# The beginning of a layer rebuilt: the first norm's scale spread by TensorE, the rotary tables computed on GpSimd, half of the key-value product between the indexer's blocks

## The chip, the cores and the metric

The kernel runs on one core of a Trainium2 chip. A core has five engines, each with an instruction stream of its own that runs in order: TensorE (PE, matmuls and transposes), VectorE (DVE), ScalarE (ACT), GpSimd (POOL) and SyncE (SP, which here issues the DMAs). They wait for each other through semaphores. The metric is the time of one execution on the device in microseconds (us); the median of several runs is given.

## The reference

The input (512 tokens of width 1024, float32) goes through a first layer norm and then through two hybrid decoder layers, each of which is, cut to what matters:

```python
x = layer_norm(x, ln_in_g, ln_in_b)            # once, ahead of both layers
h = x @ w_in                                   # 1704 columns: qa ka va qb kb vb qi ki wi
qa, ka, qb, kb, qi = (rope(...) for each)      # rotary by cos/sin of position * frequency
ki = rope(layer_norm(ki, idx_k_g, idx_k_b))
oa = swa_sink_attention(qa, ka, va, sinks)     # window of 128, 8 heads, 2 key heads
score = sum_h relu(qi_h . ki) * wi_h           # the indexer: 8 heads of width 32
sel = top_k(causal score, 128)
ob = attention of qb over the selected kb, vb  # 8 heads, 1 key head
x = layer_norm(ALPHA * x + concat(oa, ob) @ w_o, ln1_g, ln1_b)
ffn = (silu(x @ w_g) * (x @ w_u)) @ w_down     # 2816 wide
ple = (p @ w_pp) * sigmoid(x @ w_pg)
x = layer_norm(ALPHA * x + ffn + ple, ln2_g, ln2_b)
```

## The kernel before

**Tiles.** The 512 tokens are four tiles of 128 (x0 to x3, on partitions). `to_features(t)` turns a tile by eight PE transposes (L340), and ACT and DVE write it as a high half `fh` (L342) and a low half `fl` (L343). Every product is done in float32 as three matmuls of halves (`mm3`: L252 high by high, L253 high by low, L254 low by high).

**Weights.** SP loads a piece of weights into one of three `wst` buffers; ACT casts its high half (L228) and POOL subtracts for the low half (L229) into one of five `wsp` buffers. `w_pump` does this ahead of use, and `w_rel` gives a buffer back once the last product that uses it has been written.

**The beginning of a layer.** In layer 0, `ln_in(t)` norms a tile: statistics (L301, L306), the inverse root by a few operations on one column (L283 to L293), and two passes of multiply and add with scale and shift (`lng`, `lnb`), which are loaded as rows spread over 128 partitions. Tile 0 does this in two DVE operations of 1024 columns (L309, L316); tiles 1 to 3 do the first pass's upper half on POOL (L311, L312) and the rest on DVE (L313, L319). `rotary()` computes the angles of all positions, takes them down to one period by fourteen DVE operations (L370, L371, L376), and fills the tables `tab64` and `tab32` after ACT's sines (L379, L380). `start()` then does, for each tile, the 296 columns of the indexer ("the group": 24 matmuls a tile), then the 384 columns of keys and values ("key-value", tiles 0 and 1 first, then 2 and 3: 48 matmuls each), and two blocks of queries. In layer 1 the tiles 0 to 2 are turned at the end of layer 0 and only tile 3 is turned in `start()`.

**What follows.** Each product is rotated: `rope` multiplies by the table on DVE (L402), adds the halves (L404), then ACT makes the high half (L407) and POOL the low one (L408). `turn` transposes the result on PE (L414), and ACT copies it out (L415). `index()` multiplies index queries and keys for tiles 1, 2 and 3 (eight matmuls each of 256, 384 and 512 columns, L547), ACT takes the relu, and DVE accumulates in `work` (L550). `topk()` then finds the 128 largest of every row in sixteen rounds of eight (L561, L562) and makes the mask (L564), on DVE; the sparse attention of a tile waits for it. The attention runs after, and `w_o` closes the stretch.

**What sets the order.** `Order.run` interleaves streams that yield their PE cost; `later` puts a turn off by some microseconds of it. The code order that this gives is then rearranged by the framework's scheduler, engine by engine, so the final order of an engine isn't the order of the code. All PSUM tiles share eight banks.

## Time and profile before

| | |
|---|---|
| median of 3 runs | 1331.31 us (1329.1 to 1331.56) |
| the profiled execution | 1331.07 us |
| its span | 1329.2 us |
| PE busy | 1269.0 us (95%) |
| DVE busy | 620.0 us (47%) |
| POOL busy | 563.5 us (42%) |
| ACT busy | 510.6 us (38%) |

The span is what the profiler recorded of that execution, from the first to the last instruction; the execution's own time is 1.87 us longer. The busy shares are means over stages of very different kind: in the feed-forward part PE alone is full, while in the stretch from the start to `w_o` several engines are. The rows further down are of that stretch. [...]

### The profile page before, as it was taken

The numbers are of one execution on the slowest core, as the hardware profiler recorded it, in microseconds if no ns is written. First come the engines' busy times: TensorE is split into PE (matmuls) and PEld (weight loads), VectorE is DVE, ScalarE is ACT, GpSimd is POOL, SyncE is SP. The second block draws the span as 40 slices with busy tenths as digits, with TensorE's granted clock in tenths as the row PEclk, the third lists the DMA queues.
The fourth block names the chain that finished last, engine by engine and source line by source line (L and its number), as shares of the span: only waits on it lengthen the run. The fifth ranks groups of instructions, "written<-read, shape, count | busy, mean of one in ns | idle before, by whom it ended". The sixth has DMA issues, their size and how long they took to land.

```text
span 1329.2 us, 17760 instructions
## 1 busy us (share of the span) xinstructions
PE 1269.0 (95%) x6744; PEld 1098.4 (83%) x6744; DVE 620.0 (47%) x1532; ACT 510.6 (38%) x1052; POOL 563.5 (42%) x366
## 2 busy tenths in 40 slices
PE   2899999999999999999998999999999999999996
PEld 2899889788888888888897998989888888888885
DVE  7899956812120012122688998674121102121166
ACT  1566766333221132223246576743232212222220
POOL 5565332344444444443055534324444444444422
PEclk9899999999999999999998999998999999999999
DMA  5322110233332332234032210204333333232221
GB/s 183 95 80 70 44 33 32 84 100 102 96 111 95 95 95 96 95 96 136 19 105 84 91 33 33 64 13 130 96 98 100 117 97 95 96 95 95 95 79 48
DMA packets 88645, 113.77 MB, mean 86 GB/s; under 512 B 4848, under 2 KB 65264, under 8 KB 88560
## 3 DMA queue, kind: packets, MB, share of 16 engines
q1 hardware_dynamic: 88560, 112.64, 26.6%
q8 instruction: 53, 0.87, 0.3%
q14 instruction: 32, 0.26, 0.1%
HBM read 110.53 MB, written 2.10 MB: 85 GB/s over the span
## 4 chain that ended last, share of the span: by engine, by line
PE 85%; DVE 12%; ACT 1%; issue 1%; DMA 1%; SPq 0%; DVEq 0%; ACTq 0%
PE bank L252 26%; PE bank L253 26%; PE bank L254 26%; PE bank L586 2%; PE bank L630 2%; DVE t2k L404 2%; DVE work L562 1%; DVE m L561 1%; DVE t2k L402 1%; PE bank L624 1%; DVE t2k L589 1%; PE bank L547 1%; PE bank L414 1%; DVE fl L343 1%; DVE x L332 1%
## 5 line engine op out<-in xcount | busy, mean ns | idle before, releaser
L229 POOL TENSOR_TENSOR wsp<-wst,wsp 128x1024 fp32r<-128x1024 f32 (+2 forms) x190 | 450.7, 2377 | 535.7 <-ACT wsp L228 535.4
L228 ACT CAST wsp<-wst 128x1024 fp32r<-128x1024 f32 (+2 forms) x190 | 194.6, 1027 | 459.9 <-PE bank L254 288.8
L253 PE MATMUL bank<-fl,wsp 128*128 128x512 f32 (+1 forms) x768 | 286.9, 374 | 1.7 <-DVE fl L343 1.7
L254 PE MATMUL bank<-fh,wsp 128*128 128x512 f32 (+1 forms) x768 | 286.6, 374 | 0.0
L252 PE MATMUL bank<-fh,wsp 128*128 128x512 f32 (+1 forms) x768 | 285.4, 375 | 1.0 <-ACT fh L342 1.0
L786 DVE TENSOR_TENSOR t2k<-bank,t2k 128x512 f32<-128x512 f32 x44 | 30.0, 691 | 356.5 <-PE bank L254 356.5
L252 PE MATMUL bank<-wsp,slot 128*128 128x512 f32 x432 | 169.2, 392 | 0.0
L253 PEld LDWEIGHTS bank<-fl,wsp 128*128 128x128 f32 x768 | 146.7, 191 | 27.2 <-DVE fl L343 2.2
L254 PE MATMUL bank<-wsp,fl 128*128 128x256 f32 (+3 forms) x512 | 165.6, 325 | 3.5 <-DVE fl L343 3.5
L253 PE MATMUL bank<-wsp,slot 128*128 128x512 f32 x432 | 168.2, 389 | 0.0
L254 PE MATMUL bank<-wsp,slot 128*128 128x512 f32 x432 | 168.1, 389 | 0.0
L252 PE MATMUL bank<-wsp,fh 128*128 128x256 f32 (+3 forms) x512 | 166.8, 329 | 0.9 <-ACT fh L342 0.5
L252 PEld LDWEIGHTS bank<-fh,wsp 128*128 128x128 f32 x768 | 145.4, 191 | 26.5 <-ACT fh L342 1.9
L254 PEld LDWEIGHTS bank<-fh,wsp 128*128 128x128 f32 x768 | 146.6, 191 | 25.0
L253 PE MATMUL bank<-wsp,fh 128*128 128x256 f32 (+3 forms) x512 | 165.8, 324 | 0.1
L254 PEld LDWEIGHTS bank<-wsp,fl 128*128 128x128 f32 x512 | 99.2, 194 | 9.2 <-DVE fl L343 4.2
L252 PEld LDWEIGHTS bank<-wsp,fh 128*128 128x128 f32 x512 | 98.8, 194 | 7.9 <-ACT fh L342 1.4
L253 PEld LDWEIGHTS bank<-wsp,fh 128*128 128x128 f32 x512 | 99.5, 194 | 5.8 <-POOL wsp L229 0.4
L254 PEld LDWEIGHTS bank<-wsp,slot 128*128 128x128 f32 x432 | 81.1, 188 | 16.9
L253 PEld LDWEIGHTS bank<-wsp,slot 128*128 128x128 f32 x432 | 81.1, 188 | 16.2
L252 PEld LDWEIGHTS bank<-wsp,slot 128*128 128x128 f32 x432 | 81.1, 188 | 16.1
L707 DVE SCALAR_TENSOR_TENSOR x<-x,bank 128x512 f32<-128x512 f32 x32 | 21.8, 684 | 117.5 <-PE bank L254 117.5
(150 smaller groups left out, 1737.4 us busy)
## 6 DMA issues: line engine op xcount, KB each, us to landing
wst<-in_w_gu_dram SPq DMA_DIRECT2D x88, 512.0 KB, 3.4
wst<-in_w_down_dram SPq DMA_DIRECT2D x44, 512.0 KB, 3.6
wst<-in_w_in_dram SPq DMA_DIRECT2D x16, 512.0 KB, 3.5
wst<-in_w_o_dram SPq DMA_DIRECT2D x16, 512.0 KB, 3.6
wst<-in_w_pg_dram SPq DMA_DIRECT2D x16, 512.0 KB, 3.7
wst<-in_w_in_dram SPq DMA_DIRECT2D x8, 296.0 KB, 4.0
x<-in_x_dram SPq DMA_DIRECT2D x4, 512.0 KB, 8.7
wst<-in_w_in_dram SPq DMA_DIRECT2D x8, 256.0 KB, 2.8
```

The lines of the kernel that those rows point to most:

```text
L228: A.copy(w[:, 0, :a * n], st[:, :a * n])
L229: G.tensor_tensor(w[:, 1, :a * n], st[:, :a * n], w[:, 0, :a * n], OP.subtract)
L252: PE.matmul(o, sh, mh, start=start, stop=False)
L253: PE.matmul(o, sh, ml, start=False, stop=False)
L254: PE.matmul(o, sl, mh, start=False, stop=stop)
L332: V.scalar_tensor_tensor(xt[t], xt[t], rs, b_t, op0=OP.mult, op1=OP.add)
L343: V.tensor_tensor(fl[:, 4 * j:4 * j + 4, ts], pv, fh[:, 4 * j:4 * j + 4, ts], OP.subtract)
L404: V.tensor_tensor(t1.rearrange("p n (u i) -> p n u i", u=2), t1.rearrange("p n (u i) -> p n u i", u=2), t2.rearrange("p n (u i) -> p n u i ...
L586: PE.matmul(ps[:, o:o + nn], qT[kind, t, g][:, j * 128:(j + 1) * 128], kT[c, s][:, k0:k0 + nn], start=(s == 0), stop=(s == 1))
L630: PE.transpose(ps[:, j * 128:(j + 1) * 128], es[j][:, b * 128:(b + 1) * 128], idf)
L707: V.scalar_tensor_tensor(xt[t][:, c], xt[t][:, c], scale, ps, op0=OP.mult, op1=OP.add)
L786: V.tensor_tensor(b, ps[1, f], a, OP.mult)
```

## The change

- **Loads.** The positions and frequencies go first, x0 comes in two halves, and the first norm's scale and shift come as two tiles of 8 by 128 (`gb8`), in place of two rows spread over 128 partitions. x1 to x3 are issued inside `w_pump`, behind weight pieces 1, 3 and 4 (`X_AT`). The group's weights come in three pieces (3, 3 and 2 blocks of 128 rows) instead of four. The small rows of the indexer's norm and the sinks are issued after the rotary.
- **First norm.** Sixteen matmuls of a column of the identity, broadcast, by `gb8` put scale and shift on all partitions in four PSUM banks. `ln_in` does every tile in four DVE operations of 512 columns that read those banks; POOL has no part in it any more. `ln_apply` stays for the last norm only.
- **Rotary.** All its reduction runs on POOL, each multiply-add as two operations (24 in place of DVE's 14), and the table copies go from POOL to ACT.
- **Order of a layer's beginning.** The key-value product of tiles 0 and 1 runs after the group of tile 1 (layer 0) or of tile 2 (layer 1), ahead of the remaining groups. The key-value weights of the upper four row blocks go into `slot` tiles, their low halves still by POOL. `ln_in(t + 1)` is issued after tile t has been turned. `project` now takes weight pieces of unequal length and is told how many of them to give back.
- **ln1's scale** (`load_gb(("1", l))`) is loaded ahead of the attention rather than after it, held in the order of the program.

```diff
@@ -139,22 +139,26 @@
     def load_x(t):
-        SP.dma_start(xt[t], x[0, t * 128:(t + 1) * 128, :])
-    load_x(0)
+        for c in (slice(0, 512), slice(512, D)) if t == 0 else (slice(0, D),):
+            SP.dma_start(xt[t][:, c], x[0, t * 128:(t + 1) * 128, c])
     SP.dma_start(posi, bass.AP(tensor=positions.tensor, offset=positions.offset, ap=[[1, 128], [128, NT]]))
     bcast_row(invf, inv_freq, 0, 48)
+    load_x(0)
+    gb8 = t2k()
+    for i, row in enumerate((ln_in_g, ln_in_b)):
+        SP.dma_start(gb8[:KT, i * 128:(i + 1) * 128],
+                     bass.AP(tensor=row.tensor, offset=row.offset, ap=[[128, KT], [1, 128]]))
     gb = {}
     def load_gb(key, g_ap, b_ap, off):
...
         b_t = const.tile([128, D], F32, name="lnb", tag="lnb")
-        bcast_row(g_t, g_ap, off, D)
-        bcast_row(b_t, b_ap, off, D)
+        for dst, src in ((g_t, g_ap), (b_t, b_ap)):
+            tc.keep_in_program_order(bcast_row(dst, src, off, D))
         gb[key] = (g_t, b_t)
-    load_gb("in", ln_in_g, ln_in_b, 0)
-    load_x(1)
     wq = []
@@ -168,10 +172,10 @@
     for l in range(L):
+        for k, a in ((0, 3), (3, 3), (6, 2)):
+            plan(a, rows(w_in[l], k, a, QI, NIN))
         for k in range(0, KT, 2):
-            plan(2, rows(w_in[l], k, 2, QI, NIN))
-        for k in range(0, KT, 2):
-            plan(2, rows(w_in[l], k, 2, KA, KA + 256), rows(w_in[l], k, 2, KB, KB + 128))
+            plan(2, rows(w_in[l], k, 2, KA, KA + 256), rows(w_in[l], k, 2, KB, KB + 128), extra=k >= 4 and G)
         for c in (QA, QA + 256, QB, QB + 256):
@@ -209,6 +214,8 @@
                 wst_live[wpos["dma"]] = st
+                if wpos["dma"] in X_AT:
+                    load_x(X_AT[wpos["dma"]])
                 wpos["dma"] += 1
@@ -217,10 +224,10 @@
                 if extra:
-                    w = [[slot() for _ in range(a)] for _ in range(2)]
+                    w = [[slot()[:, :n] for _ in range(a)] for _ in range(2)]
                     for k in range(a):
                         A.copy(w[0][k], st[:, k * n:(k + 1) * n])
-                        V.tensor_tensor(w[1][k], st[:, k * n:(k + 1) * n], w[0][k], OP.subtract)
+                        extra.tensor_tensor(w[1][k], st[:, k * n:(k + 1) * n], w[0][k], OP.subtract)
                     w_live[i] = w
@@ -264,10 +267,16 @@
     V.tensor_copy(win[:, 128:], causal[:, S - 128:])
...
+    gb_in = []
+    for i in range(2):
+        for j in range(2):
+            ps = bank("gb", 4)
+            for k in range(KT // 2):
+                PE.matmul(ps[:, k * 128:(k + 1) * 128], idf[:KT, 4 * j + k, None].to_broadcast([KT, 128]),
+                          gb8[:KT, i * 128:(i + 1) * 128], start=True, stop=True)
+            gb_in.append(ps)
     def tok(t):
@@ -300,25 +309,30 @@
         V.bn_stats(stats[t][:, h, :], xt[t][:, h * 512:(h + 1) * 512])
...
+    def ln_in(t):
+        mv = sm(2, "bmv")
+        for h in range(2):
+            ln_stats(t, h)
+        V.bn_aggr(mv, stats.pop(t))
+        halves = [xt[t][:, h * 512:(h + 1) * 512] for h in range(2)]
+        for h, c in enumerate(halves):
+            V.scalar_tensor_tensor(c, c, mv[:, 0:1], gb_in[h], op0=OP.subtract, op1=OP.mult)
+        rs = rstd_of(mv[:, 1:2])
+        for h, c in enumerate(halves):
+            V.scalar_tensor_tensor(c, c, rs, gb_in[2 + h], op0=OP.mult, op1=OP.add)
@@ -342,15 +356,8 @@
             V.tensor_tensor(fl[:, 4 * j:4 * j + 4, ts], pv, fh[:, 4 * j:4 * j + 4, ts], OP.subtract)
-    def ln_in(t):
-        for h in range(2):
-            ln_stats(t, h)
-        ln_apply(t, "in")
-    ln_in(0)
-    V.tensor_copy(posf, posi)
+    G.tensor_copy(posf, posi)
...
     def rotary():
         n = NT * 48
...
+        ang, kk, aa, pr = t2k(), t2k(), t2k(), t2k()
         a3 = ang[:, :n].rearrange("p (t f) -> p t f", t=NT)
...
         for period, bits, terms in ((2 * math.pi * 4096, 7, 6), (2 * math.pi, 11, 4)):
-            V.tensor_scalar(kk[:, :n], ang[:, :n], 1.0 / period, magic, op0=OP.mult, op1=OP.add)
-            V.tensor_scalar(kk[:, :n], kk[:, :n], magic, None, op0=OP.subtract)
+            G.tensor_scalar(kk[:, :n], ang[:, :n], 1.0 / period, magic, op0=OP.mult, op1=OP.add)
+            G.tensor_scalar(kk[:, :n], kk[:, :n], magic, None, op0=OP.subtract)
             rest = period
...
                 rest -= c
-                V.scalar_tensor_tensor(ang[:, :n], kk[:, :n], -c, ang[:, :n], op0=OP.mult, op1=OP.add)
+                G.tensor_scalar(pr[:, :n], kk[:, :n], -c, None, op0=OP.mult)
+                G.tensor_tensor(ang[:, :n], pr[:, :n], ang[:, :n], OP.add)
         lim = 3.1415925
@@ -383,12 +391,18 @@
         for tab, f0, h in ((tab64, 0, 32), (tab32, 32, 16)):
-            G.tensor_copy(tab[:, :, 0, :h], c3[:, :, f0:f0 + h])
-            G.tensor_copy(tab[:, :, 0, h:], c3[:, :, f0:f0 + h])
-            G.tensor_copy(tab[:, :, 1, :h], s3[:, :, f0:f0 + h])
+            A.copy(tab[:, :, 0, :h], c3[:, :, f0:f0 + h])
+            A.copy(tab[:, :, 0, h:], c3[:, :, f0:f0 + h])
+            A.copy(tab[:, :, 1, :h], s3[:, :, f0:f0 + h])
             G.tensor_scalar(tab[:, :, 1, h:], s3[:, :, f0:f0 + h], -1.0, None, op0=OP.mult)
+    w_pump()
+    ln_in(0)
     rotary()
@@ -716,20 +728,21 @@
...
         def start():
-            ws = take(4)
+            gi, kv = take(3), []
             for t in range(NT):
-                if l == 0 and t > 0:
-                    ln_in(t)
                 if l == 0 or t == 3:
...
                     yield 0.9
-                yield from project(ws, 296, (t,), from_f, gi_out, t == 3)
-            ws = take(4)
-            for b in ALL:
-                yield from project(ws, 384, b, from_f, kv_out, b is ALL[-1])
+                if l == 0 and t + 1 < NT:
+                    ln_in(t + 1)
+                yield from project(gi, 296, (t,), from_f, gi_out, 3 * (t == 3))
+                if t == (1 if l == 0 else 2):
+                    kv = take(4)
+                    yield from project(kv, 384, ALL[0], from_f, kv_out)
+            yield from project(kv, 384, ALL[1], from_f, kv_out, 2)
             for q in QS[:NSTART]:
@@ -741,19 +754,19 @@
...
         order.run((start(), 1.0), (index(), 1.0))
+        load_gb(("1", l), ln1_g, ln1_b, l * D)
         order.run((rest(), R_MAIN), (attention(), 1.0), (topk(), R_TOP))
         order.flush()
-        load_gb(("1", l), ln1_g, ln1_b, l * D)
         wo = [take(2), take(2)]
```

How the order moves is seen at three places. In the rows, `x_85` to `x_88` are tiles 0 to 3, and lines of the new kernel are L354 (turn a tile to features), L255 to L257 (the three matmuls of `mm3`), L428 (turns of index queries), L525 (turns of keys), L559 (index product), L310 (statistics), L316 (their mean), L319 and L322 (the two passes of the norm).

PE of layer 0 around the first index product, before: key-value matmuls, turns, index product of tile 1, turns, index product of tile 2.

```order
L252 MATMUL bank<-wsp,fh 128x384
L253 MATMUL bank<-wsp,fh 128x384
L254 MATMUL bank<-wsp,fl 128x384
L414 MATMUL bank<-idr,slot 128x128 x10
L547 MATMUL bank<-slot 128x256 x8
L414 MATMUL bank<-idr,slot 128x128 x18
L547 MATMUL bank<-slot 128x384 x8
L252 MATMUL bank<-wsp,fh 128x384
```

The same place after the change:

```order
L255 MATMUL bank<-slot,fh 128x384
L256 MATMUL bank<-slot,fh 128x384
L257 MATMUL bank<-slot,fl 128x384
L354 MATMUL bank<-idf,x_87 128x128 x8
L428 MATMUL bank<-idr,slot 128x128 x10
L559 MATMUL bank<-slot 128x256 x8
L255 MATMUL bank<-wsp,fh 128x296
L256 MATMUL bank<-wsp,fh 128x296
L257 MATMUL bank<-wsp,fl 128x296
```

The first index product now stands right behind tile 2's transposes and half of the key-value product, and ahead of the groups of tiles 2 and 3 (the 296-column matmuls).

PE of layer 0 at the index products of tile 3, before: they stand one by one among the key-value matmuls.

```order
L253 MATMUL bank<-wsp,fh 128x384
L547 MATMUL bank<-slot 128x512
L254 MATMUL bank<-wsp,fl 128x384
L252 MATMUL bank<-wsp,fh 128x384
L253 MATMUL bank<-wsp,fh 128x384
L254 MATMUL bank<-wsp,fl 128x384
L252 MATMUL bank<-wsp,fh 128x384
L253 MATMUL bank<-wsp,fh 128x384
L547 MATMUL bank<-slot 128x512
```

After:

```order
L255 MATMUL bank<-wsp,fh 128x256
L256 MATMUL bank<-wsp,fh 128x256
L257 MATMUL bank<-wsp,fl 128x256
L428 MATMUL bank<-idr,slot 128x128 x10
L559 MATMUL bank<-slot 128x384 x8
L559 MATMUL bank<-slot 128x512 x8
L525 MATMUL bank<-idr,slot 128x128 x12
L255 MATMUL bank<-wsp,fh 128x256
L256 MATMUL bank<-wsp,fh 128x256
L257 MATMUL bank<-wsp,fl 128x256
```

The eight products of tile 2 and the eight of tile 3 now form one row, behind a block of query matmuls and ten turns.

DVE at the first norm of layer 0, before (`lng`, `lnb` are the spread rows):

```order
L306 BN_AGGR bmv<-bst 128x2
L292 TENSOR_SCALAR lnt_158<-lns_157,lnv_156 128x1
L376 SCALAR_TENSOR_TENSOR t2k<-t2k 128x192
L313 SCALAR_TENSOR_TENSOR x_86<-x_86,bmv,lng 128x512
L283 TENSOR_SCALAR lnv_263<-bmv 128x1
L293 TENSOR_SCALAR lns_157<-lnt_158,lns_157 128x1
L376 SCALAR_TENSOR_TENSOR t2k<-t2k 128x192
L286 TENSOR_SCALAR lns_264<-lnv_263 128x1
L316 SCALAR_TENSOR_TENSOR x_85<-x_85,lns_157,lnb 128x1024
L370 TENSOR_SCALAR t2k<-t2k 128x192
```

After (`bank` are the PSUM banks with scale and shift):

```order
L319 SCALAR_TENSOR_TENSOR x_85<-x_85,bmv,bank 128x512
L302 TENSOR_SCALAR lns_197<-lnt_198,lns_197 128x1
L310 BN_STATS bst<-x_86 128x6 x2
L322 SCALAR_TENSOR_TENSOR x_85<-x_85,lns_197,bank 128x512
L316 BN_AGGR bmv<-bst 128x2
L319 SCALAR_TENSOR_TENSOR x_86<-x_86,bmv,bank 128x512 x2
L292 TENSOR_SCALAR lnv_284<-bmv 128x1
L310 BN_STATS bst<-x_87 128x6 x2
L322 SCALAR_TENSOR_TENSOR x_85<-x_85,lns_197,bank 128x512
L310 BN_STATS bst<-x_88 128x6 x2
```

The statistics of tile 1 (and of tiles 2 and 3) now stand among tile 0's passes, and the rotary steps (L376, L370) are gone from between them.

## Rows read from the trace of the kernel before

**Rows 1.** The page, parts 1 and 4: busy time, share of the span and instructions of each engine; shares of the chain of work that ended last, by engine.

```profile
PE 1269.0 (95%) x6744; PEld 1098.4 (83%) x6744; DVE 620.0 (47%) x1532; ACT 510.6 (38%) x1052; POOL 563.5 (42%) x366
...
PE 85%; DVE 12%; ACT 1%; issue 1%; DMA 1%; SPq 0%; DVEq 0%; ACTq 0%
```

**Rows 2.** Windows of layer 0's first stretch: the window, its length, then busy us (instructions) of PE, PEld, DVE, ACT and POOL, PE's granted clock, the DMA share and GB/s.

```profile
20.00:40.00 20.00, 13.78 (x65) 12.08 (x64) 19.16 (x53) 5.60 (x11) 15.09 (x15) 0.91 0.38 107
40.00:60.00 20.00, 16.85 (x114) 16.68 (x114) 19.64 (x65) 8.07 (x18) 13.66 (x16) 1.00 0.35 104
60.00:80.00 20.00, 17.00 (x75) 15.09 (x76) 15.50 (x46) 13.79 (x39) 4.84 (x10) 0.74 0.10 28
160.00:180.00 20.00, 16.60 (x92) 13.48 (x93) 14.12 (x53) 14.11 (x51) 5.12 (x9) 1.00 0.08 27
```

**Rows 3.** Timeline of PE in layer 0: start, duration, engine, line, operation, operands, count, and in brackets the idle time before and what ended it.

```profile
18.08 1.97 PE L340 MATMUL bank<-idf,x 128*128 128x128 f32 x8 [18.08 <-DVE x L316]
...
24.26 0.62 PE L254 MATMUL bank<-wsp,fl 128*128 128x296 f32 x1 [3.53 <-DVE fl L343]
...
32.70 1.55 PE L340 MATMUL bank<-idf,x 128*128 128x128 f32 x8 [2.65 <-DVE x L319]
...
38.93 1.04 PE L340 MATMUL bank<-idf,x 128*128 128x128 f32 x8
...
48.26 0.34 PE L252 MATMUL bank<-wsp,fh 128*128 128x384 f32 x1
...
56.09 0.96 PE L414 MATMUL bank<-idr,slot 128*128 128x128 f32 x10
60.91 1.42 PE L547 MATMUL bank<-slot 128*128 128x256 f32 x5 [3.86 <-ACT slot L415]
```

**Rows 4.** Timeline of DVE in layer 0, same columns: x0's statistics, its first multiply, an early rotary step, its last multiply, three additions of the ropes, the first operation of topk(1) and the last one of topk(3).

```profile
4.52 1.29 DVE L301 BATCH_NORM_STATS2 bst<-x 128x6 f32<-128x512 f32 x2 [2.56 <-DMA x<-in_x_dram]
...
9.22 1.28 DVE L309 SCALAR_TENSOR_TENSOR x<-x,bmv,lng 128x1024 f32<-128x1024 f32 x1 [2.97 <-DMA lng<-in_ln_in_g_dram]
...
11.13 0.35 DVE L376 SCALAR_TENSOR_TENSOR t2k<-t2k 128x192 f32<-128x192 f32 x1
...
16.75 1.27 DVE L316 SCALAR_TENSOR_TENSOR x<-x,lns,lnb 128x1024 f32<-128x1024 f32 x1
...
47.83 3.83 DVE L404 TENSOR_TENSOR t2k<-t2k 128x64 f32<-128x64 f32 x3
...
66.55 0.43 DVE L561 MAX8 m<-work 128x8 f32<-128x256 f32 x1
...
170.41 0.43 DVE L564 TENSOR_SCALAR work<-work 128x512 f32<-128x512 f32 x1
```

**Rows 5.** Waits of PE in 690:830 (layer 1): engine, line, what it waited for, us in total, times, longest.

```profile
PE bank L547 <- ACT slot L415: 5.0, 1, 5.0
```

**Rows 6.** Windows of layer 1's first stretch, columns as in rows 2.

```profile
700.00:720.00 20.00, 14.69 (x75) 13.09 (x74) 16.60 (x57) 12.55 (x36) 7.69 (x13) 0.74 0.16 50
708.00:712.00 4.00, 3.71 (x20) 2.77 (x19) 3.27 (x8) 3.30 (x10) 0.00 (x0) 0.50 0.00 0
712.00:716.00 4.00, 4.00 (x16) 3.52 (x15) 3.40 (x11) 3.94 (x12) 1.33 (x3) 0.50 0.00 0
800.00:820.00 20.00, 17.99 (x113) 15.22 (x111) 19.74 (x69) 15.43 (x54) 9.85 (x14) 1.00 0.16 54
```

**Rows 7.** The page, part 6: DMA issues of the x tiles, count, KB each, median us from issue to landing.

```profile
x<-in_x_dram SPq DMA_DIRECT2D x4, 512.0 KB, 8.7
```

**Rows 8.** Timeline of ACT in layer 0, columns as in rows 3: the two fh casts of x2.

```profile
39.57 1.07 ACT L342 CAST fh<-bank 128x512 fp32r<-128x512 f32 x2 [0.25 <-PE bank L340]
```

**Rows 9.** Groups of DVE's instructions in 0:66, by line and shape: busy us, mean ns of one, idle time before them.

```profile
L376 DVE SCALAR_TENSOR_TENSOR t2k<-t2k 128x192 f32<-128x192 f32 x10 | 7.8, 776 | 0.0
...
L343 DVE TENSOR_TENSOR fl<-bank,fh 128x512 fp32r<-128x512 f32 x8 | 5.4, 678 | 0.6 <-ACT fh L342 0.6
...
L319 DVE SCALAR_TENSOR_TENSOR x<-x,lns,lnb 128x512 f32<-128x512 f32 x6 | 4.9, 869 | 0.0
```

**Rows 10.** Groups of POOL's instructions in 0:56, same columns.

```profile
L311 POOL TENSOR_SCALAR x<-x,bmv 128x512 f32<-128x512 f32 x3 | 5.6, 1882 | 0.4 <-DVE bmv L306 0.4
...
L312 POOL TENSOR_TENSOR x<-x,lng 128x512 f32<-128x512 f32 x3 | 3.8, 1272 | 0.0
...
L381 POOL TENSOR_TENSOR t2k<-t2k 128x192 f32<-128x192 f32 x1 | 0.5, 501 | 0.0
...
L382 POOL TENSOR_SCALAR t2k<-t2k 128x192 f32<-128x192 f32 x1 | 0.4, 352 | 0.1
```

**Rows 11.** Timeline of POOL in layer 0, columns as in rows 3: a weight split.

```profile
46.96 2.00 POOL L229 TENSOR_TENSOR wsp<-wst,wsp 128x768 fp32r<-128x768 f32 x1 [0.54 <-ACT wsp L228]
```

**Rows 12.** Groups of DVE's instructions in 60:100, columns as in rows 9.

```profile
L550 DVE SCALAR_TENSOR_TENSOR work<-bank,wi,work 128x512 f32<-128x512 f32 x7 | 5.2, 741 | 0.0
L550 DVE SCALAR_TENSOR_TENSOR work<-bank,wi,work 128x384 f32<-128x384 f32 x7 | 4.2, 606 | 0.0
...
L404 DVE TENSOR_TENSOR t2k<-t2k 128x128 f32<-128x128 f32 x4 | 1.4, 341 | 0.0
```

**Rows 13.** Waits of PE in 66:180, columns as in rows 5.

```profile
PE bank L547 <- DVE work L550: 1.4, 2, 0.9
```

**Rows 14.** Groups of POOL's instructions in 80:100, columns as in rows 9.

```profile
L229 POOL TENSOR_TENSOR wsp<-wst,wsp 128x1024 fp32r<-128x1024 f32 x6 | 14.6, 2449 | 6.8 <-ACT wsp L228 6.8
```

More of the change, by code (lines that the diff above doesn't have):

```diff
@@ L191, in hybrid_kernel @@
             for k in range(0, KT, 2):
-                plan(2, rows(w_pg[l], k, 2, h * 512, (h + 1) * 512), extra=h == 1)
-            plan(2, rows(w_pp[l], 0, 2, h * 512, (h + 1) * 512), extra=h == 1)
+                plan(2, rows(w_pg[l], k, 2, h * 512, (h + 1) * 512), extra=h == 1 and V)
+            plan(2, rows(w_pp[l], 0, 2, h * 512, (h + 1) * 512), extra=h == 1 and V)
     wst_live, w_live = {}, {}
     W_AHEAD, ST_AHEAD = 5, 3
+    X_AT = {1: 1, 3: 2, 4: 3}
     wpos = dict(dma=0, split=0, use=0, room=W_AHEAD)
@@ L301, in ln_stats, with ln_apply @@
         V.bn_stats(stats[t][:, h, :], xt[t][:, h * 512:(h + 1) * 512])
-    def ln_apply(t, key, last=False):
+    def ln_in(t):
[9 more added lines that the diff above has]
+            V.scalar_tensor_tensor(c, c, rs, gb_in[2 + h], op0=OP.mult, op1=OP.add)
+    def ln_apply(t, key):
         g_t, b_t = gb[key]
@@ L424, in take, with project @@
         return [w_take() for _ in range(n)]
-    def project(ws, n, blocks, lhs, done, last, nk=KT):
-        a = nk // len(ws)
+    def project(ws, n, blocks, lhs, done, rel=0):
+        ks = [(i, r, len(w[0])) for i, w in enumerate(ws) for r in range(len(w[0]))]
         ps = [acc() for _ in blocks]
-        for k in range(nk):
-            wh, wl = (ws[k // a][r][k % a] for r in range(2))
-            for i, t in enumerate(blocks):
-                xh, xl = lhs(t, k)
-                mm3(ps[i][:, :n], xh, xl, wh, wl, k == 0, k == nk - 1)
-            if last and k % a == a - 1:
+        for k, (i, r, a) in enumerate(ks):
+            for o, t in zip(ps, blocks):
+                mm3(o[:, :n], *lhs(t, k), ws[i][0][r], ws[i][1][r], k == 0, k == len(ks) - 1)
+            if i < rel and r == a - 1:
                 w_rel()
             yield 3 * len(blocks) * 0.218 * n / 512
-        for i, t in enumerate(blocks):
-            done(t, ps[i])
+        for o, t in zip(ps, blocks):
+            done(t, o)
     for l in range(L):
@@ L855, in hybrid_kernel @@
                         if h == 1:
-                            ln_apply(t, ("2", l), l == L - 1)
+                            ln_apply(t, ("2", l))
                     else:
```

35 lines of the change are left out of this document (12 added, 23 removed).

## The prediction

> **What bounds the kernel now.** I read the page's first and fourth parts first. TensorE (PE) is busy for 1269.0 of 1329.2 us and owns 85% of the chain of work that ended last; VectorE (DVE) owns 12% [rows 1]. The change takes no matmul away, so it can only win idle time of PE, or time in which PE ran at half its clock. It touches what comes before the output projection of each layer, so I then read the 20 us windows of that stretch. In layer 0 PE loses 6.2 us in 20:40, 3.2 in 40:60, 3.0 in 60:80 and 3.4 in 160:180, while DVE is busy for over 19 of 20 us from 20 to 60 [rows 2]. Two engines are near their limit at once: a microsecond given to PE alone comes back as a wait for DVE later.
>
> The timeline of PE names the losses. PE starts 18.08 us late, behind x0's norm; it waits 3.53 us for the low half of x0's features at 24.26, 2.65 for x1 at 32.70, and 3.86 for the turned index queries at 60.91 [rows 3]. On DVE the norm begins at 4.52, idles 2.97 for the broadcast scale (lng) at 9.22 and ends 1.27 after 16.75; the first top-k operation is at 66.55, the last one at 170.41 [rows 4]. Layer 1 has the same pause ahead of its first index product, 5.0 us [rows 5], and behind it PE runs at a granted clock of 0.50, the lower of its two levels [rows 6].
>
> **The start.** Two 512 KB broadcasts become two loads of 4 KB, and sixteen small matmuls spread them over four PSUM banks. PE is idle then, so they cost nothing; without that cover they would cost what sixteen transposes do, 3.9 us by 1.97 for eight [rows 3]. DVE no longer idles for lng. But the order puts x1's BN_STATS, which waits for x1's load, ahead of x0's last multiply. An x load takes 8.7 us to land [rows 7]; x1's is issued ninth, behind two weight pieces, which I estimate at 2.7 us, so x1 lands near 11.4. Then 1.3 for its statistics and 0.7 for the multiply make x0's lower half ready near 13.5. The upper half stands behind x1's two multiplies (1.4), x2's statistics (1.3) and its own 0.7: near 17. Half the transposes (1.0), the copy (0.5, of 1.07 for two [rows 8]) and the low half (0.68 [rows 9]) give a first low-half matmul near 19.7 (with 0.5 for hand-overs) instead of 24.26: **-4.5 us**. If x1 lands 2 us later it is -2.5; if it lands at 9, -7.
>
> x0's group then ends at 25.5 (it took 24.26 to 32.70 less the pause, 5.8), and x1 is normed near 27.3, as its upper half no longer goes through GpSimd (POOL): a pause of 1.8 in place of 2.65, **-0.9** (0 to -2.6).
>
> **DVE and POOL.** Fourteen rotary operations leave DVE; ten of them, at L376, took 7.8 us in all, though one undisturbed takes 0.35 [rows 4, 9]. The norm brings back three upper halves of about 0.7 each, so DVE is relieved by 5 to 7 us. On POOL the rotary is now 24 more operations: by the nearest rows (0.50 with two inputs, 0.35 with one, same shape) 10 x 0.50 + 14 x 0.35 = 9.9 us; the POOL halves of the norm that go took 3 x (1.88 + 1.27) = 9.5 [rows 10]. POOL comes out even.
>
> The two engines disturb each other: three additions at L404 took 3.83 us at 47.83 [rows 4], beside a weight split that POOL began at 46.96 [rows 11], where 0.341 is the mean of one in 60:100 [rows 12]. Operations that read PSUM did not stretch (L343 0.678, while L319, all from SBUF, took 0.869 [rows 9]), so I put the norm's multiplies, which now read PSUM, at 0.7. [...]
>
> [...]
>
> **The new wait ahead of the first index product.** PE now does x1's group (6.2 us from 32.70 to 38.93, its transposes with it), half the key-value product (7.8 from 48.26 to 56.09 [rows 3]) and x2's transposes: 27.3 + 6.2 + 7.8 + 1.0, about 42. Next in its order come the turns of t1's index queries. These need the rotated queries, these the tables, and the last four table copies stand on ScalarE (ACT) behind x2's fh casts (1.07 for two [rows 8]) and behind POOL's long chain. So the tables are whole near 44; then come DVE's low halves of x2 (2 x 0.68), t1's ropes and additions and POOL's low halves, with the keys' ropes among them: turns near 49, a pause of about 7 where 3.86 stood, **+3 us** (0 if the tables come by 40; +8 if the additions stretch as at 47.83). Index 1 runs near 50 instead of 60.91 and topk(1) starts about 10 us sooner; but t2, t3 and the second key-value half are still to come, so part of this lead is only order.
>
> **The index products of t2 and t3.** Before, t3's eight are strewn among key-value and query matmuls. Now all sixteen stand in PE's order with nothing between. Each needs a bank, hence DVE's accumulation at L550: 8 x 0.606 + 8 x 0.741 = 10.8 us [rows 12], while PE needs about 3.0 for them (estimate: 7.8 / 48 = 0.163 for 384 columns, 0.217 for 512). PE can run ahead by about six of the eight banks, worth 4. So 3.8 us of wait replace the 1.4 that it waits for L550 now [rows 13]: **+2.4** (-1.4 to +6.4, with no banks ahead). The clock's loss behind a pause (0.74 granted in 60:80 [rows 2]) stays as it is in the sum, since a pause of this size stands there before and after.
>
> **The end of layer 0's stretch.** PE's 3.4 us of loss in 160:180 come while DVE works off topk(3) until 170.41 [rows 2, 4]. With DVE relieved and topk(1) sooner, I put that end 6 to 9 us earlier, and most of the loss goes: **-3** (0 to -3.4). Layer 0: -4.5 - 0.9 + 3 + 2.4 - 3 = **-3.0**.
>
> **Layer 1** has no first norm and no rotary. Here half the key-value product runs ahead of index 1 and x3's group after it, so that DVE can rope t1 meanwhile. At most the wait of 5.0 [rows 5] goes and, of 708:716 at 0.50, half of the 7.71 us of PE work [rows 6], 3.9: -8.9. But DVE idles only 3.4 us of 700:720, and it is still full in 800:820 (19.74 of 20), where PE waits for it (17.99) [rows 6]. So DVE allows about -3.4, and the row of fifteen index products may cost up to 6.4 again. I take **-2.5**, with -7 to +3 as bounds.
>
> The other edits go together at 0: the longer weight pieces carry the same bytes, the earlier loads of ln1's scale take a queue that is behind its buffers anyway, hidden by the attention's PE work until that norm; uncovered they would cost one load's 7 to 9 us.
>
> **Sum.** -3.0 - 2.5 = -5.5. The profiled execution took 1331.07 (span 1329.2 and 1.87 around it), so 1325.6; the median of the runs is 0.24 higher, 1325.8, and I say **1326**. About 0.2% (2.7 us) is what a measurement of this kernel can tell from no change.
>
> **The rivals.** (a) DVE decides, no change: the gain at the start is spent waiting for ropes (+6 instead of +3) and the end's loss hardly shrinks (-1); layer 0 is -4.5 - 0.9 + 6 + 2.4 - 1 = +2.0, layer 1 -2: 1331. For it: DVE is full in most windows [rows 2]; against it: 5 to 7 us of its work really leave. (b) The gain carries through: the tables are ready when PE asks (-2), the row of index products is covered (0), the end's loss goes (-3.4), so layer 0 is -4.5 - 0.9 - 2 - 3.4 = -10.8, and layer 1 -3.4 as far as DVE allows: 1317. For it: POOL's sum comes out even. (c) Slower, one mechanism: weights held back. The five wsp buffers hold three first pieces and two key-value pieces until x3's group ends, so the query weights are split late, three splits of 2.449 us each [rows 14] back to back, ahead of the ropes' low halves for t3. Then 7.3 us of splits come onto PE's path, and the row of index products costs its whole +6.4: layer 0 is -4.5 - 0.9 + 3 + 6.4 + 7.3 - 3 = +8.3, layer 1 -1: 1338. It decides once the two pauses together exceed some 11 us, the gains of the start, the end and layer 1. Against it: x3's group and the second key-value half, over 10 us of PE work, can cover the splits. (d) The first norm doesn't start sooner because x1's load is late: the start is then -2.5, which lies within the forecast's range.
>
> **How the numbers follow.** Forecast (1320.5 to 1328.4) 0.45; (a), within 0.2%, 0.22; (b) 0.13; (c) 0.20. The range 1315 to 1337 leaves out the low end of (b) and the upper half of (c). Faster by over 0.2%: 0.45 + 0.13 = 0.58; within it 0.22; slower 0.20.
>
> **What would show it.** Right: the first low-half matmul near 19.7; index 1 near 50 behind a pause of some 7 us; the row of sixteen index products with PE waiting for DVE's accumulation; topk(3) done by 161 to 165; in layer 1 no pause ahead of index 1. Wrong: layer 0's first output-projection matmul later than now, or PE waiting for POOL's splits.

## The result and the profile after

The change makes the kernel slower: 1349.71 us median (1348.03 to 1350.63) against 1330.71 (1329.1 to 1331.56) of the kernel before, a ratio of 1.0143 with a 95% interval of 1.0125 to 1.016. Medians and ratios here and below leave out two slow executions, one of run 4 below (1989.0 us at a mean granted clock of 0.6) and one of run 11 (1439.66 at 0.84); all others have 0.969 to 0.987. The span of the profiled execution is 1346.3 us. Parts 1 and 4 of the page, as in [rows 1]:

```profile
PE 1279.5 (95%) x6776; PEld 1103.7 (82%) x6776; DVE 625.3 (46%) x1522; ACT 511.3 (38%) x1060; POOL 565.7 (42%) x381
...
PE 80%; DVE 15%; ACT 2%; issue 1%; DMA 1%; POOL 0%; DVEq 0%; SPq 0%; POOLq 0%; ACTq 0%
```

PE is busy 10.5 us longer, and its share of the chain falls from 85% to 80%, while DVE's rises from 12% to 15%. The extra busy time holds 7.2 us of the new matmuls that spread the scale; low-clock stretches add to it. The granted clock is the share of TensorE's full speed that the profile shows as granted: of the 1329 windows of 1 us of the kernel before it is 1.00 in 1283, 0.50 in 33 and between these in 13; of the 1346 of the new kernel it is 1.00 in 1279, 0.50 in 56 and between these in 11. In 98:100, at 0.50, a query matmul of 256 columns starts every 0.21 us, and in 72:74, at 1.00, every 0.12. The windows of layer 0 (columns as in [rows 2]):

```profile
20.00:40.00 20.00, 16.88 (x104) 15.97 (x102) 15.06 (x61) 6.53 (x18) 16.83 (x26) 1.00 0.36 100
40.00:60.00 20.00, 13.62 (x83) 13.20 (x84) 15.30 (x49) 10.19 (x41) 6.11 (x11) 0.74 0.00 1
80.00:100.00 20.00, 15.48 (x53) 10.78 (x54) 17.29 (x48) 14.23 (x46) 4.83 (x9) 0.50 0.00 1
160.00:180.00 20.00, 17.34 (x123) 15.67 (x122) 17.29 (x66) 16.52 (x56) 11.10 (x14) 1.00 0.19 54
```

PE has gained in 20:40 (16.88 for 13.78), but in 80:100 it is busy for 15.48 us at a granted clock of 0.50 throughout, where the kernel before had a full window at 1.00:

```profile
80.00:100.00 20.00, 19.97 (x163) 19.57 (x162) 19.34 (x54) 14.58 (x47) 17.67 (x16) 1.00 0.44 132
```

The timeline of PE (as in [rows 3]) shows what stands ahead of that:

```profile
17.92 0.62 PE L257 MATMUL bank<-wsp,fl 128*128 128x296 f32 x1 [0.32 <-DVE fl L357]
...
24.66 1.38 PE L354 MATMUL bank<-idf,x 128*128 128x128 f32 x8 [1.77 <-DVE x L322]
...
44.09 1.51 PE L428 MATMUL bank<-idr,slot 128*128 128x128 f32 x10 [5.34 <-POOL slot L422]
47.65 2.07 PE L559 MATMUL bank<-slot 128*128 128x256 f32 x8 [2.06 <-ACT slot L429]
...
83.52 1.51 PE L428 MATMUL bank<-idr,slot 128*128 128x128 f32 x10 [8.72 <-POOL slot L422]
85.39 1.33 PE L559 MATMUL bank<-slot 128*128 128x384 f32 x3 [0.36 <-ACT slot L429]
```

The start is better than before: the first low-half matmul is at 17.92 (24.26), x1's transposes at 24.66 (32.70), the first index product at 47.65 (60.91). Then PE waits 8.72 us at 83.52 for the turns of tile 3's index keys, and the second index product is at 85.39. In the kernel before it stands at 66.49:

```profile
66.49 1.88 PE L547 MATMUL bank<-slot 128*128 128x384 f32 x6
```

What PE waited for is on DVE (as in [rows 4]): the statistics of tile 3's index key, the first operation of topk(1) behind it, the additions of its queries' ropes, two steps of the keys' inverse root, the ropes of the keys, and the last operation of topk(3).

```profile
65.30 0.19 DVE L468 BATCH_NORM_STATS2 kst<-bank 128x6 f32<-128x32 f32 x1
...
66.14 0.42 DVE L573 MAX8 m<-work 128x8 f32<-128x256 f32 x1
...
66.55 3.54 DVE L418 TENSOR_TENSOR t2k<-t2k 128x128 f32<-128x128 f32 x2
...
71.70 2.29 DVE L295 TENSOR_SCALAR lns<-lnv 128x2 int32<-128x2 int32 x1
...
74.30 2.62 DVE L297 TENSOR_SCALAR lnv<-lnv 128x2 f32<-128x2 f32 x1
...
81.65 0.28 DVE L416 TENSOR_TENSOR t2k<-kin,tab 128x128 f32<-128x128 f32 x1
...
171.93 0.41 DVE L576 TENSOR_SCALAR work<-work 128x512 f32<-128x512 f32 x1
```

From the statistics to the rope of the keys pass 16.4 us. The same stretch of the kernel before, from its timeline of DVE:

```profile
51.59 0.18 DVE L456 BATCH_NORM_STATS2 kst<-bank 128x6 f32<-128x32 f32 x1
...
59.22 0.29 DVE L402 TENSOR_TENSOR t2k<-kin,tab 128x128 f32<-128x128 f32 x1
```

There it is 7.6. In the new kernel two things lie in between: rounds of topk(1) (0.9 us each), which before began only after these keys were done, and operations that take many times their length, among them 2.29 and 2.62 for operations on two columns (0.16 and 0.15 in run 5 below). The timeline of POOL says what ran beside these:

```profile
62.76 7.19 POOL L236 TENSOR_TENSOR wsp<-wst,wsp 128x1024 fp32r<-128x1024 f32 x3 [3.02 <-ACT wsp L235]
...
71.56 4.72 POOL L236 TENSOR_TENSOR wsp<-wst,wsp 128x1024 fp32r<-128x1024 f32 x2 [0.17 <-ACT wsp L235]
```

They are the splits of the first five query weight pieces (a split is the subtraction that makes the low half of a weight piece). Layer 1, which has neither first norm nor rotary, shows the same (windows, and waits of PE in 690:780; before: [rows 6] and [rows 5]):

```profile
700.00:720.00 20.00, 18.28 (x115) 16.99 (x113) 15.55 (x53) 12.06 (x32) 8.89 (x13) 0.91 0.00 1
720.00:740.00 20.00, 11.16 (x81) 10.69 (x80) 19.83 (x54) 6.05 (x22) 11.73 (x11) 0.79 0.44 131
740.00:760.00 20.00, 18.33 (x98) 13.89 (x98) 19.54 (x44) 14.82 (x41) 7.03 (x9) 0.78 0.01 2
```

```profile
PE bank L428 <- ACT slot L527: 8.4, 1, 8.4
```

The 5.0 us ahead of the first index product are gone, and 8.4 us ahead of the second one have come, with a low clock behind them (0.78 in 740:760). How much each layer loses is read at two places of PE's timeline: a turn of a tile behind ln1, the norm that follows layer 0's output projection, and the first of these matmuls of layer 1's output projection. Before:

```profile
252.91 1.09 PE L340 MATMUL bank<-idf,x 128*128 128x128 f32 x8 [1.72 <-DVE lns L286]
...
815.39 0.39 PE L252 MATMUL bank<-wsp,slot 128*128 128x512 f32 x1
```

After:

```profile
260.48 1.09 PE L354 MATMUL bank<-idf,x 128*128 128x128 f32 x8 [1.72 <-DVE lns L295]
...
832.39 0.39 PE L255 MATMUL bank<-wsp,slot 128*128 128x512 f32 x1
```

That is +7.6 at the first place and +17.0 at the second: layer 0 loses 7.6 us, layer 1 another 9.4.

### The profile page after: what moved, and what is told of

Same layout as the page of the kernel before. It is cut to its first block, busy times and chain, and to the rows that moved or that the text cites. A ratio compares the mean times of both kernels' runs of the same rounds, so it can differ in the third digit from the quotient of the medians.

```text
span 1346.3 us, 17883 instructions
## 1 busy us (share of the span) xinstructions
PE 1279.5 (95%) x6776; PEld 1103.7 (82%) x6776; DVE 625.3 (46%) x1522; ACT 511.3 (38%) x1060; POOL 565.7 (42%) x381
## 4 chain that ended last, share of the span: by engine, by line
PE 80%; DVE 15%; ACT 2%; issue 1%; DMA 1%; POOL 0%; DVEq 0%; SPq 0%; POOLq 0%; ACTq 0%
PE bank L255 25%; PE bank L256 25%; PE bank L257 25%; DVE work L574 3%; DVE m L573 2%; PE bank L598 2%; DVE t2k L418 1%; PE bank L642 1%; DVE work L562 1%; DVE t2k L601 1%; DVE t2k L416 1%; DVE x L346 1%; DVE fl L357 1%; PE bank L636 1%; PE bank L354 0%
## 5 line engine op out<-in xcount | busy, mean ns | idle before, releaser
L236 POOL TENSOR_TENSOR wsp<-wst,wsp 128x1024 fp32r<-128x1024 f32 (+2 forms) x184 | 441.7, 2405 | 539.2 <-ACT wsp L235 539.2
L235 ACT CAST wsp<-wst 128x1024 fp32r<-128x1024 f32 (+2 forms) x184 | 190.4, 1040 | 462.6 <-PE bank L257 290.2
L257 PE MATMUL bank<-fh,wsp 128*128 128x512 f32 (+1 forms) x768 | 285.5, 372 | 0.0
L255 PE MATMUL bank<-fh,wsp 128*128 128x512 f32 (+1 forms) x768 | 284.1, 373 | 1.0 <-ACT fh L356 1.0
L255 PE MATMUL bank<-wsp,slot 128*128 128x512 f32 x432 | 169.4, 392 | 0.0
L257 PE MATMUL bank<-wsp,slot 128*128 128x512 f32 x432 | 168.2, 389 | 0.0
L255 PEld LDWEIGHTS bank<-fh,wsp 128*128 128x128 f32 x768 | 144.2, 189 | 26.5 <-ACT fh L356 1.9
L257 PEld LDWEIGHTS bank<-fh,wsp 128*128 128x128 f32 x768 | 145.4, 189 | 25.1
L255 PE MATMUL bank<-wsp,fh 128*128 128x256 f32 (+3 forms) x480 | 156.7, 327 | 0.2 <-ACT fh L356 0.2
L257 PE MATMUL bank<-wsp,fl 128*128 128x256 f32 (+3 forms) x480 | 154.3, 323 | 0.3 <-DVE fl L357 0.3
L256 PE MATMUL bank<-wsp,fh 128*128 128x256 f32 (+3 forms) x480 | 154.3, 322 | 0.0
L255 PEld LDWEIGHTS bank<-wsp,fh 128*128 128x128 f32 x480 | 93.6, 195 | 6.0 <-ACT fh L356 0.9
L257 PEld LDWEIGHTS bank<-wsp,fl 128*128 128x128 f32 x480 | 93.0, 194 | 5.7 <-DVE fl L357 0.7
L256 PEld LDWEIGHTS bank<-wsp,fh 128*128 128x128 f32 x480 | 93.6, 195 | 4.8
L257 PEld LDWEIGHTS bank<-wsp,slot 128*128 128x128 f32 x432 | 81.1, 188 | 17.0
L255 PEld LDWEIGHTS bank<-wsp,slot 128*128 128x128 f32 x432 | 81.1, 188 | 16.1
L422 POOL TENSOR_TENSOR slot<-t2k,slot 128x256 fp32r<-128x256 f32 (+1 forms) x64 | 44.3, 708 | 84.0 <-ACT slot L421 76.3
```

What stands on the lines that cost most here:

```text
L235: A.copy(w[:, 0, :a * n], st[:, :a * n])
L236: G.tensor_tensor(w[:, 1, :a * n], st[:, :a * n], w[:, 0, :a * n], OP.subtract)
L255: PE.matmul(o, sh, mh, start=start, stop=False)
L256: PE.matmul(o, sh, ml, start=False, stop=False)
L257: PE.matmul(o, sl, mh, start=False, stop=stop)
L422: G.tensor_tensor(lo, s, hi, OP.subtract)
```

## The experiments

All edits are to the changed kernel unless said otherwise, and each diff is cut to its main lines. Theory O: the earlier first index product lets topk(1) onto VectorE ahead of tile 3's index keys. Theory W: the splits of the query weights on GpSimd now stand beside these keys and stretch VectorE. Rival S: the moved rotary and the new norm cost the time. Ratios are against the kernel before.

**1. The order taken back.**

```diff
-                if t == (1 if l == 0 else 2):
-                    kv = take(4)
-                    yield from project(kv, 384, ALL[0], from_f, kv_out)
+            kv = take(4)
+            yield from project(kv, 384, ALL[0], from_f, kv_out)
             yield from project(kv, 384, ALL[1], from_f, kv_out, 2)
```

> The changed kernel with only the place of the first key-value block taken back (it runs after the groups of all four tiles, in both layers); norm, rotary, loads and weight pieces stay. Theory O (the earlier first index product lets topk(1) onto VectorE ahead of t3's index keys) and theory W (the splits of the query weights on GpSimd then stand beside t3's index keys and stretch VectorE): both place the whole loss in this order, so the time falls below the kernel before, 1322 to 1328 us, with no pause of PE over 5 us ahead of the second index product. Rival S (rotary on GpSimd and first norm by PE cost the time): layer 0 keeps its +7.6, 1336 or more.

1328.39 us, ratio 0.9983 (0.9971 to 0.9995), 0.4 above the range that was written. The order makes the loss, some 21 us; S falls.

**2. The order alone, in the kernel before** (its plan of weight pieces, `project`, `start` and the place of `load_gb(("1", l))` taken over; norm, loads and rotary as they were).

> The kernel before with only the key-value block moved (with the weight pieces, slot tiles and load of ln1's scale that it needs); norm, rotary and loads as before. O and W: slower than before by about as much as the whole change or more, 1345 to 1355 us, with a pause of PE of 8 us or so ahead of the second index product in both layers. S: 1329 to 1333.

1359.74, ratio 1.0216 (1.02 to 1.0232), above the range that was written. The new norm, loads and rotary win 10 us back from this order, but only 2.5 from the old one (run 1 against before).

**3. The order in layer 1 alone.**

```diff
-                if t == (1 if l == 0 else 2):
+                if t == (3 if l == 0 else 2):
```

> The changed kernel with the key-value order taken back in layer 0 alone. If the loss is the same mechanism in each layer, half of the 21 us between the change and the kernel with the order taken back in both stays: 1337 to 1341. If it is layer 0's (its VectorE also has the first norm): 1329 to 1333; if layer 1's: 1346 or more.

1338.56, ratio 1.0061 (1.0043 to 1.0079): about half of the 21 us stay. That fits one mechanism, once in each layer.

**4. topk(1) held.** `keyed[3]` is the addition that ropes the index keys of tiles 2 and 3.

```diff
-                    V.max(m8, w)
+                    with tc.issue_after(keyed[3]) if t == 1 and r == 0 else nullcontext():
+                        V.max(m8, w)
```

> The changed kernel with the first operation of topk(1) held, on VectorE's queue, behind the addition that ropes the index keys of tiles 2 and 3; nothing else. O: t3's keys are turned some 5 us sooner and the pause of PE ahead of the second index product shrinks from 8.7 to 3 or less, 1349.7 falls by 8 to 14 us, to about 1338. W: the splits still stand beside t3's index keys, the pause stays over 6 us, 1345 or more.

1345.48, ratio 1.0114 (1.0097 to 1.0131): 4 us, half of the least that O said. The keys are turned 4.6 us earlier, but the pause has only moved. PE in this kernel:

```profile
78.88 1.04 PE L429 MATMUL bank<-idr,slot 128*128 128x128 f32 x10 [2.55 <-DVE work L576]
84.44 1.33 PE L560 MATMUL bank<-slot 128*128 128x384 f32 x3 [4.53 <-ACT slot L430]
```

2.55 us ahead of the turns, then 4.53 for ACT's copies of them, which stand in ACT's queue behind casts of the key-value ropes that DVE now reaches late.

**5. Five splits off.** `nolo` holds the first five query weight pieces of each layer.

```diff
-                    G.tensor_tensor(w[:, 1, :a * n], st[:, :a * n], w[:, 0, :a * n], OP.subtract)
+                    if i in nolo:
+                        A.copy(w[:, 1, :a * n], st[:, :a * n])
+                    else:
+                        G.tensor_tensor(w[:, 1, :a * n], st[:, :a * n], w[:, 0, :a * n], OP.subtract)
```

> The changed kernel with the low halves of the first five query weight pieces of each layer left out (ACT writes a copy of the high half instead, so those queries are wrong), so that GpSimd has nothing beside t3's index keys. W: the three stretched VectorE operations there (3.5, 2.3 and 2.6 us) fall to 0.6 or less each, the pause ahead of the second index product falls to 2 us or less, 8 to 14 us less in all, about 1338. O: topk(1)'s rounds still stand ahead, the pause stays over 5 us, 1345 or more.

1336.3, ratio 1.0047 (1.003 to 1.0064): 13.4 us less, as W said. DVE at the same place (the two additions, the two steps of the inverse root, the keys' rope between the first and the last line):

```profile
69.54 0.18 DVE L474 BATCH_NORM_STATS2 kst<-bank 128x6 f32<-128x32 f32 x1
...
70.84 0.46 DVE L424 TENSOR_TENSOR t2k<-t2k 128x128 f32<-128x128 f32 x2
...
72.18 0.16 DVE L301 TENSOR_SCALAR lns<-lnv 128x2 int32<-128x2 int32 x1
...
72.64 0.15 DVE L303 TENSOR_SCALAR lnv<-lnv 128x2 f32<-128x2 f32 x1
...
76.36 0.29 DVE L422 TENSOR_TENSOR t2k<-kin,tab 128x128 f32<-128x128 f32 x1
```

0.46, 0.16 and 0.15 where 3.54, 2.29 and 2.62 stood. 8 us are left to run 1.

**6. Both.** Runs 4 and 5 in one kernel.

> The changed kernel with topk(1) held behind the ropes of the index keys of tiles 2 and 3 and, besides, the low halves of the first five query weight pieces of each layer left out (a copy by ACT stands for them, so those queries are wrong). With the splits alone off, 1336.3 was measured, 8 above the same kernel with the key-value order taken back. O (topk(1) overtaking makes up the rest): 1328 to 1331. P (the rest is the later place of the groups of tiles 2 and 3, which no order on VectorE mends): 1334 or more, and the turns of t3 still later than 74 us where they were at 59 in the kernel with the order taken back.

1328.38, ratio 0.9982 (0.9972 to 0.9991): as with the order taken back. The groups of tiles 2 and 3 still come late in it, and the turns of tile 3 start at 76.15, later than 74 as P said; the time of P, 1334 or more, did not come. PE no longer waits ahead of them.

```profile
68.49 0.20 DVE L475 BATCH_NORM_STATS2 kst<-bank 128x6 f32<-128x32 f32 x1 [9.25 <-PE bank L263]
...
72.72 0.29 DVE L422 TENSOR_TENSOR t2k<-kin,tab 128x128 f32<-128x128 f32 x1
```

Runs 4 to 6 make a square. From the statistics to the keys' rope, in layer 0 and in layer 1 (the difference of two starts on DVE):

| | splits beside | splits off |
|---|---|---|
| topk(1) ahead | 16.4, 16.6 | 6.8, 7.9 |
| topk(1) held | 9.3, 9.3 | 4.2, 4.2 |

Alone the rounds add 2.6 to 3.7 us to this chain and the splits 5.1; together they add 12. With both, the chain lasts longer, so more rounds and more splits fall into it.

The time of the kernel reads otherwise. Over run 6, the rounds alone cost 7.9 us (run 5), the splits alone 17.1 (run 4) and both 21.3 (the change): less than their sum. So the length of the chain is not the price. In run 4 the chain of layer 0 is 7.1 us shorter than in the change, and yet the turn behind ln1 comes at 261.05, where the change has 260.48. The splits also cost where this chain is not.

One comparison is missing: no run takes the splits off in the old order. Run 1 has them beside tile 3's keys too; the chain there takes 11.7 us in layer 0, with operations of 2.42 and 2.41, and 9.5 in layer 1. So run 6 matches a kernel that still pays for splits, and a few us that the new place itself costs are not excluded.

**7. The splits later, all computed.** All key-value weights go to slot tiles, so two query pieces are split early; the next three wait on POOL for the low half of tile 3's index keys.

```diff
-            plan(2, rows(w_in[l], k, 2, KA, KA + 256), rows(w_in[l], k, 2, KB, KB + 128), extra=k >= 4 and G)
+            plan(2, rows(w_in[l], k, 2, KA, KA + 256), rows(w_in[l], k, 2, KB, KB + 128), extra=G)
...
-                yield from project(gi, 296, (t,), from_f, gi_out, 3 * (t == 3))
+                yield from project(gi, 296, (t,), from_f, gi_out)
+                if t == 3:
+                    with tc.issue_after(keyed[3]):
+                        for _ in range(3):
+                            w_rel()
```

> The changed kernel, computing all of it: the key-value weights all go to slot tiles, so that two query pieces are split before the first index product, and the three that follow tile 3's group are held on GpSimd behind the low half of t3's index keys. W (the splits beside t3's index keys cost 13 us): as with the five splits off, 1334 to 1340, and the three stretched VectorE operations fall to 0.6 us or less each. Rival (the splits are only moved, PE then waits for the weights of the next query block): 1345 or more, with a wait of PE for GpSimd's wsp.

1355.75, ratio 1.0191 (1.0174 to 1.0208), worse than the change. PE:

```profile
48.64 1.51 PE L428 MATMUL bank<-idr,slot 128*128 128x128 f32 x10 [9.01 <-POOL slot L422]
...
85.01 0.69 PE L559 MATMUL bank<-slot 128*128 128x384 f32 x1 [3.02 <-DVE slot L518]
87.77 3.57 PE L559 MATMUL bank<-slot 128*128 128x384 f32 x5 [2.08 <-DVE work L562]
96.87 3.36 PE L559 MATMUL bank<-slot 128*128 128x512 f32 x7 [5.53 <-ACT slot L429]
```

At tile 3's keys it does what W said: the chain takes 9.6 us instead of 16.4, and the pause ahead of their turns falls to 0.71. But the two early splits delay the rotary tables (a pause of 9.01 ahead of the first index product, 5.34 in the change), and the late ones now stand beside the key-value ropes; the second and third index products wait in turn (3.02, 2.08 and 5.53). PE does not wait for the weights themselves: the rival's time was right, its reason was not.

**8. The splits in quarters, all computed.** `fine` holds the query weight pieces.

```diff
-                    G.tensor_tensor(w[:, 1, :a * n], st[:, :a * n], w[:, 0, :a * n], OP.subtract)
+                    step = 256 if i in fine else a * n
+                    for c0 in range(0, a * n, step):
+                        c = slice(c0, min(c0 + step, a * n))
+                        G.tensor_tensor(w[:, 1, c], st[:, c], w[:, 0, c], OP.subtract)
```

> The changed kernel with each split of a query weight piece on GpSimd cut into four of 256 columns; the order on the engines stays, all is computed. If a VectorE operation beside a split waits out the whole GpSimd instruction: the three stretched operations at t3's index keys (3.5, 2.3 and 2.6 us) fall to about 0.9, 0.6 and 0.6, the pause of 8.7 ahead of the second index product falls to about 3, and the time to 1337 to 1343. Rival (what counts is the total time that GpSimd reads, so VectorE gets its turn only when the burst ends): the stretches stay within 1 us in sum and the time over 1346.

1341.06, ratio 1.0072 (1.0059 to 1.0085): 8.7 us less, with the same work in the same order on DVE and POOL at this place. DVE:

```profile
66.28 0.19 DVE L474 BATCH_NORM_STATS2 kst<-bank 128x6 f32<-128x32 f32 x1
...
67.53 1.25 DVE L424 TENSOR_TENSOR t2k<-t2k 128x128 f32<-128x128 f32 x2
...
70.38 0.41 DVE L301 TENSOR_SCALAR lns<-lnv 128x2 int32<-128x2 int32 x1
...
71.11 0.39 DVE L303 TENSOR_SCALAR lnv<-lnv 128x2 f32<-128x2 f32 x1
...
77.39 0.46 DVE L422 TENSOR_TENSOR t2k<-kin,tab 128x128 f32<-128x128 f32 x1
```

1.25, 0.41 and 0.39 instead of 3.54, 2.29 and 2.62, and 11.1 us from the statistics to the keys' rope instead of 16.4. The pause ahead of the turns is 4.53, where about 3 was written. POOL works longer than before on the same five splits (14.2 us in 20 instructions, 11.9 in five), so here the stretch follows the length of the single POOL instruction (0.71 us in the mean, 2.38 before) and not POOL's total.

**9. Quarters and topk(1) held** (runs 4 and 8 in one kernel).

> The same, with topk(1) held behind the ropes of the index keys of tiles 2 and 3 as well. With splits off and topk(1) held 1328.4 was measured; if the quarters free VectorE, this computes all and comes to 1328 to 1336; if not, 1343 or more, as held alone.

1346.14, ratio 1.0107 (1.0094 to 1.012): not free, and 5 us worse than the quarters alone, although the chain is shorter (7.8 us, 11.1 in run 8). DVE is now idle for 6.66 us ahead of tile 3's group, the held rounds stand among the key-value ropes, and PE waits 3.41 us behind the turns. With whole splits the same hold won 4 us (run 4), so its worth depends on what else stands there.

**10. The old order with the rotary back on DVE** (run 1 with `rotary` and its table copies as before).

> The changed kernel with the key-value order taken back in both layers and the rotary back on VectorE (its table copies back on GpSimd): the first norm, loads and weight pieces stay. If the rotary on GpSimd is worth something in the old order: 1331 to 1335, 3 to 6 above the 1328.4 with it. If the norm alone makes the gain: 1327 to 1330.

1330.83, ratio 1.0003 (0.9993 to 1.0013), 2.4 above run 1 and between the two ranges that were written; the two intervals overlap by little. The rotary's move seems to make about all that the new start is worth in the old order, but the difference is close to noise.

**11. The old order with all splits of the input projection in quarters.**

> The changed kernel with the key-value order taken back in both layers, and all splits of the input projection's weights on GpSimd cut to 256 columns. If quarters free VectorE here too (additions of the ropes beside splits): 1322 to 1327, against 1328.4 whole; if not, 1327 to 1331.

1330.13, ratio 0.9985 (0.9972 to 0.9998), as run 1: quarters win nothing in this order, although run 1 has stretched operations beside splits. Why is not shown.

**12. The old order with all key-value weights in wsp.**

```diff
-            plan(2, rows(w_in[l], k, 2, KA, KA + 256), rows(w_in[l], k, 2, KB, KB + 128), extra=k >= 4 and G)
+            plan(2, rows(w_in[l], k, 2, KA, KA + 256), rows(w_in[l], k, 2, KB, KB + 128), extra=False)
...
-            yield from project(kv, 384, ALL[1], from_f, kv_out, 2)
+            yield from project(kv, 384, ALL[1], from_f, kv_out, 4)
```

> The changed kernel with the key-value order taken back in both layers and all key-value weights back in wsp buffers. With half of them in slot tiles, layer 1 paused 7.8 us ahead of its first index product, where 5.0 stood before. If the slot tiles' four splits of 384 columns are the cause: the pause falls to about 5 and the time to 1324 to 1327; if not, 1328 to 1331.

1323.15, ratio 0.9937 (0.9924 to 0.995): faster than both kernels. The wait of PE in 660:790 and the additions of tile 3's ropes on DVE, run 1 first:

```profile
PE bank L559 <- ACT slot L429: 7.8, 1, 7.8
```

```profile
695.85 4.64 DVE L418 TENSOR_TENSOR t2k<-t2k 128x128 f32<-128x128 f32 x2
```

Run 12:

```profile
PE bank L559 <- ACT slot L429: 5.9, 1, 5.9
```

```profile
693.46 3.31 DVE L418 TENSOR_TENSOR t2k<-t2k 128x128 f32<-128x128 f32 x2
```

The pause falls from 7.8 to 5.9. But the slot tiles' splits were done before that place in run 1. What changes is what the freed buffers take in: three query pieces (1024 columns) are split there in run 1, three key-value pieces (768) in run 12, and the additions beside them take 4.64 and 3.31. The slots, meant to make room, brought longer splits to this place. But it explains the smaller part of the 5 us: by the two places of PE's timeline above, run 12 is 3.2 us ahead of run 1 behind layer 0 (246.77 for 249.92) and 3.5 at the output projection of layer 1 (809.68 for 813.22), so layer 1 gives only 0.4 of it. In layer 0 the chain of tile 3's keys takes 5.9 us where run 1 has 11.7, which fits the same cause; that it is the cause there is not shown.

## Why the prediction was wrong

- **The start** was right in mechanism and its gain put too small: 17.92 instead of 19.7, so -6.3 and not -4.5. x1's statistics ran at 10.54 without a wait, so x1 landed before the 11.4 of the estimate; its load was issued at 4.42, where 2.7 was put, an estimate that no row of the kernel before gives. The sixteen matmuls took 7.2 us and not 3.9, and still cost nothing, as the transposes of x0's upper half waited for DVE until 16.00. x1's pause came as put (1.77 for 1.8).
- **The pause ahead of the first index product** came out right in size, in part by luck: 5.34 and 2.06 for "about 7", and index 1 at 47.65 for "near 50". The tables were whole at 40.1 and not near 44, and for tables by 40 the prediction had no longer pause at all; PE was through with x2's transposes at 38.8 and not at 42, and the ropes behind the tables still took the rest. The prices on POOL were too low: twelve operations of one step took 0.69 and ten additions 0.60, not 0.35 and 0.50 (below), 15.0 us in all instead of 9.9.
- **The step that failed** is "The index products of t2 and t3", at +2.4, with the sentence ahead of it that part of topk(1)'s lead "is only order". I priced the row of sixteen products by DVE's accumulation, once they start, and never asked when their keys are ready: the sum has no term for that wait. They start at 85.39, 19 us later than before, behind a pause of 8.72 and at half clock to 100. Tile 3's keys are a chain of some twenty small DVE operations; topk(1), now runnable earlier, is interleaved with it, and the query splits, whose buffers the same tile's group and the key-value block give back, run beside it: 16.4 us where the kernel before has 7.6. I had the row that shows the second (the additions of 3.83 at 47.83, [rows 4]) and used it only as the upper bound of another wait.
- **"The end of layer 0's stretch", -3**, failed with it: topk(3) ends at 171.93, not at 161 to 165, and PE still loses 2.7 of 20 us in 160:180.
- **Layer 1, -2.5**, was +9.4 by the timelines: the 5.0 us pause went as said, and the same pause as in layer 0 took its place. That the two layers share one mechanism was open to me, and I gave it "up to 6.4".
- **Rival (c)** named the splits behind tile 3's group, and came nearest (1338); no rival reached the 1349.71. It had the splits on PE's path through POOL; but POOL stood idle for 6.12 us ahead of the low half of the keys that PE waited for (83.01), and runs 5 and 8, where absent or shorter splits shorten the VectorE operations and win 13.4 and 8.7 us, show that they act through DVE. Runs 4 to 6 settle the pause: without splits and with topk(1) held it is gone. That these two make every microsecond of the loss is not shown, as run 1 pays for splits too.
- **VectorE beside GpSimd** I priced for the norm, whose multiplies came as put (0.74 and 0.73 for 0.7), and not for the small operations of the index keys: 2.29 and 2.62 for two of them on two columns, 0.41 and 0.39 with quarter-length splits in run 8, 0.16 and 0.15 without splits in run 5. By what mechanism a split holds them up no run shows.
